# Up-projections and three branches of a gated merge are put into a queue of filling work

## The chip, the cores and the metric

The kernel runs on one NeuronCore of a Trainium2 chip. It has five engines that run side by side and wait for each other through semaphores: TensorE (PE, matrix products), VectorE (DVE), ScalarE (ACT), GpSimd (POOL) and SyncE (SP, which issues most of the transfers). The 16 DMA engines move data between HBM and the on-chip memory. The metric is the device time of one execution in microseconds (us); lower is better.

## The reference, cut to what matters

Two blocks are chained over a sequence of 1024 tokens and a model width of 1024. The first is a hybrid layer: one normalised input h feeds four branches of width 256 (a gated delta rule, "dn"; an attention with low-rank queries and keys, "mla"; a gated linear attention, "gla"; an attention with forget gates, "fox"), and a gated merge adds them up:

```python
cq = rms_norm(mla_cq, mla_q_norm)
b_q = (cq @ mla_w_q_up).reshape(b_sz, s_len, HEADS, MLA_NOPE + MLA_ROPE)
ckv = rms_norm(mla_ckv, mla_kv_norm)
b_kv = (ckv @ mla_w_kv_up).reshape(b_sz, s_len, HEADS, MLA_NOPE + MLA_V)
...
for i in range(N_BRANCHES):
    gate = jax.nn.sigmoid(h @ w_gate[i] + b_gate[i])
    merged = merged + gate * (branches[i] @ w_branch_up[i])
x = x + rms_norm(merged @ w_out, norm_mix_post)
```

An MLP follows. The second block starts from a recurrence over a separate context of 256 tokens (ctx), which needs nothing of the first block:

```python
hk = rms_norm_2(ctx, norm_g[l]) * (1.0 + scale_k) + shift_k
vk = jnp.einsum('btd,de->bte', hk, lp['w_in'][:, :BRANCH_W])
_, state_k = rglru(vk, lp, h0)
```

`rglru` is a short convolution, two gates, a decay and a scan, in two directions. Its end state starts the scan over the 1024 tokens later on.

## The kernel before, in words

Every dense product is made of three matmuls, since each operand is split into a rounded high part and the rest as a low part: hi·hi, hi·lo, lo·hi (`mm3_steps`, lines 411 to 413). A tile is 128 rows by 512 columns of one PSUM buffer; names say which pool it is from: `mm` (two buffers, and a third in turn outside the attentions) and `pp` (five). Weights come as raw tiles `wr` (128x1024, 512 KB), which ScalarE casts to `wh` (line 367) and VectorE subtracts to `wl` (line 368); three of each exist. Tiles of 128x1024 ("S") exist 32 times.

The stages are emitted one after the other: the input norm and `h`, the rows of gates, the projections of mla (`mla_proj`), the queue (`fillers`), the two attentions, the delta rule in two halves (`dn_half`), `gla`, a load ahead of the first merged branch (`prefetch`), the context path (`ctx`), the merge, the product with w_out, the MLP, and the mixers of the second block.

Two things set the order of instructions on each engine. The first is the queue of filling work, `self.fill`: generators of dense products from h that nobody needs yet, in this order: the dn projections (two halves), the gla projections, and `rest`, the products of all four gates (4 branches by 8 blocks by 48 matmuls, whose results go through a tanh to HBM as `gt`). The stages call `W(us)` wherever TensorE would wait; it takes steps off the queue until the credit of so many us is used up (one step of three matmuls of 512 columns counts 0.64), and `need(name)` runs what is left of one entry. The second is a scheduler that reorders instructions by readiness; what it gives is a fixed order on every engine, so that an instruction which waits holds up all that stands behind it on its engine.

In `mla_proj`, `up(i)` makes the 4 blocks of queries by 2 halves (8 pieces of 6 matmuls), then come 4 pieces of keys (3 matmuls) and 8 of values (3 short matmuls of 256 columns). The results are split and stored to HBM by `stage` through tiles `sth`, `stl` and `vst` (a pool of 6). `attention` reads them back.

In the context path `cx` is the loaded context; squares of it are summed over partitions by a matmul with ones (line 463), and it becomes `kh`, `kl`. Then four chunks: a weight tile (`xw`, `xwh`, `xwl`), 24 short matmuls, a copy `cv`, the convolution on VectorE, the split into `xh`, `xl`, 12 short matmuls with `abh`, `abl` (6 for each direction). After the chunks come decays and scans. Between the parts, `W(WC * us)` puts filling work.

`merge` goes over the branches in the order 3, 1, 0, 2. For each of 16 units of a branch it loads the gate `g`, makes 6 matmuls from `br`, multiplies on VectorE (line 1346) and adds into `ma` (line 1348, on VectorE or GpSimd). Branch 2 also splits each sum into `m`.

Of the kernel before, what the change touches and what calls it, by code (L numbers as in the profile page):

```python
# [9 lines left out]
F32R = mybir.dt.float32r  # L10
# [7 lines left out]
P = 128  # L18
# [9 lines left out]
WA, WB, WD, WI, WL, WS, WH, WG, WC = 1.2, 0.7, 10, 18, 0.6, 0.7, 3, 1.2, 2  # L28
# [273 lines left out]
class Build:  # L302
# [517 lines left out]
    def mla_proj(self):  # L820
# [38 lines left out]
        wq = self.load_w(self.A["wq"])  # L859

        def up(i):
            return lambda epi: self.proj(self.cols(wq, 2, 512, i), cq, epi)
# [14 lines left out]
        for hp in range(2):  # L877
            self.mla_k.append(self.stage("mk", lambda epi: self.proj(self.cols(wk, 1, 512, hp), ck, epi)))
        self.mla_v, epi = self.stage_v("mlav")
        for tb in range(8):  # L880
            hf, tl = divmod(tb, 4)
            ts = slice(tl * P, tl * P + P)
            ps = self.mm()
            self.mm3(ps[:, 0:256], [(ck.hi(0, hf)[:, ts], ck.lo(0, hf)[:, ts], wk[0][:, 256:512], wk[1][:, 256:512])])
            epi(ps, tb)

# [270 lines left out]
    def gla(self):  # L1157
        nc = self.nc
        M = nc.tensor.matmul
        self.need("gla")  # L1160
        vn = [self.S("vn") for _ in range(2)]
# [150 lines left out]
    def prefetch(self):  # L1312
        self.brs = [self.branch(b) for b in MERGE[:1]]

    def merge(self):

        nc = self.nc
        acc = Pairs(8)
        self.m = HiLo.__new__(HiLo)
        self.m.t = [None, None]  # L1320

        def finish(n, hf):
            self.hilo(acc.get(n, hf), self.m.hi(n, hf), self.m.lo(n, hf))

        last = None
        brs = self.brs
        for i, b in enumerate(MERGE):
            br = brs.pop(0)
            if i < 3 and not brs:
                brs.append(self.branch(MERGE[i + 1]))  # L1330
            for g in range(2):
                w = self.take("wup", b, g)
                split = i == 3 and g == 1
                for n, hf in sorted(((4 * g + j, hf) for j in range(4) for hf in range(2)),
                                    key=lambda v: v[::-1] if split else v):
                    c = [slice(k * HALF + (n % 4) * P, k * HALF + (n % 4) * P + P) for k in range(2)]
                    if i == 0:
                        acc.alloc(self, hf, "ma")
                    if i == 3 and self.m.t[hf] is None:
                        self.m.t[hf] = [self.S("m", F32R) for _ in range(8)]  # L1340
                    t = self.T2("g")
                    nc.sync.dma_start(t, self.gt[b, n, hf])
                    ps = self.pp() if n % 2 else self.mm()
                    self.mm3(ps, [(w[0][:, c[k]], w[1][:, c[k]], br.hi(k, hf), br.lo(k, hf)) for k in range(2)])
                    a = acc.get(n, hf)
                    nc.vector.scalar_tensor_tensor(t if i else a, t, 1.0, ps, op0=ALU.add, op1=ALU.mult)
                    if i:
                        (nc.vector if i < 3 and (n + hf) % 3 == 0 else nc.gpsimd).tensor_add(a, a, t)
                    if last:
                        finish(*last)  # L1350
                        last = None
                    if i == 3:
                        last = n, hf
        finish(*last)
# [447 lines left out]
    def rg_gates(self, v, N, c):  # L1802
# [7 lines left out]
        for d in range(2):  # L1810
# [13 lines left out]
            yield 3.6 * N / T  # L1824
# [13 lines left out]
    def rg_decay(self, st, N, c):  # L1838

        nc = self.nc  # L1840
        ms = []
        for d in range(2):
            i8 = 4 * d + c
            xc, r, ig, m = st[d]
            m = m if m is not None else self.S("m")
            nc.scalar.activation(m[:, :N], r[:, :N], AF.Tanh, scale=self.SP[:, i8:i8 + 1])
            nc.scalar.activation(r[:, :N], r[:, :N], AF.Exp, scale=self.NSP[:, i8:i8 + 1])
            nc.vector.tensor_mul(ig[:, :N], ig[:, :N], xc[:, :N])
            nc.scalar.activation(xc[:, :N], r[:, :N], AF.Square)
            nc.vector.scalar_tensor_tensor(m[:, :N], xc[:, :N], 1.0, m[:, :N], op0=ALU.add, op1=ALU.mult)  # L1850
            ms.append(m)
            yield 2.3
        return ms

    def rg_scan(self, st, ms, N, init):

        nc = self.nc
        out = []
        for d in range(2):
            xc, a, ig, _ = st[d]  # L1860
            m = ms[d]
            nc.scalar.activation(m[:, :N], m[:, :N], AF.Sqrt)
            nc.vector.tensor_mul(ig[:, :N], ig[:, :N], m[:, :N])
            f = (lambda ap: ap) if d == 0 else (lambda ap: ap[:, ::-1])
            nc.vector.tensor_tensor_scan(f(xc[:, :N]), f(a[:, :N]), f(ig[:, :N]), 0.0 if init is None else init[d],  # L1865
                                         op0=ALU.mult, op1=ALU.add)
            out.append(xc)
            yield 2.4
        return out
# [369 lines left out]
def emit(tc, ctx, A, out, dbg=None, stages=None):  # L2239
# [6 lines left out]
             ("mla", B.mla_proj), ("g0", B.fillers),  # L2246
             ("fox", B.attention), ("dn0", lambda: B.dn_half(0)),
             ("dn1", lambda: B.dn_half(1)), ("gla", B.gla),
             ("merge", B.prefetch),
# [35 lines left out]
```

## Time and profile before

| what | value |
|---|---|
| median of 3 runs | 2550.22 us (2545.32 to 2559.27) |
| profiled execution | 2546.38 us |
| its span | 2544.6 us |
| TensorE busy | 2462.2 us (97%), 12692 matmuls |
| VectorE busy | 1726.1 us (68%) |
| ScalarE busy | 1193.8 us (47%) |
| GpSimd busy | 181.9 us (7%) |
| TensorE's idle time put down to waits | largest: 10.1, 8.8, 6.5, 5.1 us by line |

The span is the part of the execution that the profiler covers; the profiled execution took 1.8 us more than it. TensorE is the bound almost everywhere, so that the time can be read as TensorE's work plus the places where it waits, or runs at a lower clock. PEclk in a window's row is the granted clock as a share of full speed, 2.4 GHz; 0.50 is the lower level, 1.2 GHz.

### The profile page before, as it was taken

What the parts mean: (1) busy time and instruction counts of PE and PEld (TensorE: products, weight loads), DVE (VectorE), ACT (ScalarE), POOL (GpSimd) and SP (SyncE); (2) the same over time, 40 slices, a digit from 0 to 9 for tenths busy, and PEclk for the clock granted to TensorE, in tenths of its full rate; (3) what the DMA queues carried; (4) which work ended last, traced back from release to release, by engine and by line L of the source; (5) the groups of instructions that cost most, each with busy time, mean ns of one, the idle gap of its engine ahead of it and who ended that gap; (6) DMA issues with size and microseconds to landing.
All of it is one profiled execution on the core that took longest, in us unless ns stands there. A gap on an engine that the chain in (4) does not pass through costs nothing. (4 is left out here: it accounts for less than half of the span.)

```text
span 2544.6 us, 33697 instructions
## 1 busy us (share of the span) xinstructions
PE 2462.2 (97%) x12692; PEld 1996.6 (78%) x12692; DVE 1726.1 (68%) x2647; ACT 1193.8 (47%) x1848; POOL 181.9 (7%) x238
## 2 busy tenths in 40 slices
PE   8989999999989999999999999999999999999997
PEld 6878898777777678877788888887888888887786
DVE  7537566574755436758867864468798999996744
ACT  6425554622514358146744543435536355445623
POOL 0000000120211111630000000000000000000000
PEclk9989999999999999999999999999999999999999
DMA  6364453584774567859676565556533333325732
GB/s 223 105 212 138 129 152 114 163 242 118 218 220 145 184 208 235 301 174 281 229 263 223 173 212 169 195 184 229 186 117 113 133 134 98 112 92 195 243 100 100
DMA packets 180084, 449.23 MB, mean 177 GB/s; under 512 B 32144, under 2 KB 42256, under 8 KB 179920
## 3 DMA queue, kind: packets, MB, share of 16 engines
q1 hardware_dynamic: 141504, 342.44, 40.7%
q0 software_dynamic: 18576, 64.63, 9.2%
q10 hardware_dynamic: 19840, 40.00, 4.2%
q8 instruction: 100, 1.64, 0.3%
q14 instruction: 64, 0.52, 0.1%
HBM read 321.55 MB, written 125.44 MB: 176 GB/s over the span
## 5 line engine op out<-in xcount | busy, mean ns | idle before, releaser
L367 ACT CAST wh<-wr 128x1024 fp32r<-128x1024 f32 (+1 forms) x243 | 254.8, 1049 | 481.6 <-PE mm L412 231.1
L368 DVE TENSOR_TENSOR wl<-wr,wh 128x1024 fp32r<-128x1024 f32 (+1 forms) x243 | 298.6, 1229 | 180.9 <-ACT wh L367 172.4
L411 PE MATMUL mm<-h,wh 128*128 128x512 f32 x736 | 301.2, 410 | 7.1 <-ACT h L467 4.3
L412 PE MATMUL mm<-h,wh 128*128 128x512 f32 x736 | 298.0, 405 | 0.0
L413 PE MATMUL mm<-h,wl 128*128 128x512 f32 x736 | 295.9, 402 | 0.3 <-DVE wl L368 0.3
L411 PE MATMUL mm<-kk,wh 128*128 128x512 f32 x704 | 275.2, 391 | 0.0
L412 PE MATMUL mm<-kk,wh 128*128 128x512 f32 x704 | 274.5, 390 | 0.5 <-DVE kk L1784 0.5
L413 PE MATMUL mm<-kk,wl 128*128 128x512 f32 x704 | 274.0, 389 | 0.0
L411 PEld LDWEIGHTS mm<-h,wh 128*128 128x128 f32 x736 | 141.8, 193 | 39.7 <-ACT h L467 5.9
L412 PEld LDWEIGHTS mm<-h,wh 128*128 128x128 f32 x736 | 141.8, 193 | 32.4 <-issue 3.6
L1994 DVE SCALAR_TENSOR_TENSOR pp<-cu,vec,pp 128x512 f32<-128x512 f32 (+9 forms) x240 | 166.7, 749 | 0.1
L413 PEld LDWEIGHTS mm<-h,wl 128*128 128x128 f32 x736 | 141.1, 192 | 32.6 <-issue 1.8
L412 PEld LDWEIGHTS mm<-kk,wh 128*128 128x128 f32 x704 | 132.1, 188 | 29.2 <-issue 1.0
L411 PEld LDWEIGHTS mm<-kk,wh 128*128 128x128 f32 x704 | 132.1, 188 | 28.3 <-issue 0.7
L413 PEld LDWEIGHTS mm<-kk,wl 128*128 128x128 f32 x704 | 132.1, 188 | 27.6 <-issue 0.2
L1512 PE MATMUL pp<-h,wh 128*128 128x512 f32 x320 | 127.1, 400 | 3.0 <-ACT x L1579 2.2
L1513 PE MATMUL pp<-h,wh 128*128 128x512 f32 x320 | 125.0, 391 | 1.4 <-DVE h L468 1.4
L1514 PE MATMUL pp<-h,wl 128*128 128x512 f32 x320 | 123.9, 390 | 0.0
L1721 PE MATMUL pp<-bl,wh 128*128 128x512 f32 x304 | 119.3, 392 | 2.3 <-DVE bl L468 1.6
L1722 PE MATMUL pp<-bh,wl 128*128 128x512 f32 x304 | 118.4, 389 | 0.0
L1720 PE MATMUL pp<-bh,wh 128*128 128x512 f32 x304 | 116.4, 391 | 1.6 <-ACT bh L472 1.6
L411 PE MATMUL mm<-cx,wh 128*128 128x512 f32 x256 | 99.8, 391 | 1.3 <-ACT cx L467 1.3
(559 smaller groups left out, 5453.2 us busy)
## 6 DMA issues: line engine op xcount, KB each, us to landing
wr<-in_wi_dram SPq DMA_DIRECT2D x77, 512.0 KB, 3.7
ws<-in_wm_dram POOLq DMA_DIRECT2D x48, 512.0 KB, 5.9
wr<-in_wo_dram SPq DMA_DIRECT2D x48, 512.0 KB, 3.7
wr<-in_wg_dram SPq DMA_DIRECT2D x32, 512.0 KB, 4.6
gt<-gt POOLq DMA_DIRECT2D x64, 256.0 KB, 3.6
g<-gt SPq DMA_DIRECT2D x64, 256.0 KB, 5.2
wm<-in_wm_dram SPq DMA_DIRECT2D x32, 512.0 KB, 5.0
br<-buB SPq DMA_DIRECT2D x32, 512.0 KB, 4.5
```

The costliest lines, as they stand in the source:

```text
L367: self.nc.scalar.copy(hi, raw)
L368: self.nc.vector.tensor_sub(lo, raw, hi.bitcast(F32))
L411: M(ps, lhsT=ah, rhs=bh, start=start and i == 0, stop=False)
L412: M(ps, lhsT=ah, rhs=bl, start=False, stop=False)
L413: M(ps, lhsT=al, rhs=bh, start=False, stop=stop and i == last)
L1512: M(ps, lhsT=ah, rhs=bh, start=start and i == 0, stop=False, skip_group_check=True)
L1513: M(ps, lhsT=ah, rhs=bl, start=False, stop=False, skip_group_check=True)
L1514: M(ps, lhsT=al, rhs=bh, start=False, stop=i == last, skip_group_check=True)
L1720: M(banks[p], lhsT=wh[:, o], rhs=bh[:, r], start=first, stop=False, skip_group_check=True)
L1721: M(banks[p], lhsT=wh[:, o], rhs=bl[:, r], start=False, stop=False, skip_group_check=True)
L1722: M(banks[p], lhsT=wl[:, o], rhs=bh[:, r], start=False, stop=jj == 7 and e == 1, skip_group_check=True)
L1994: nc.vector.scalar_tensor_tensor(o, u[:, a + s:b + s], w(j), o, op0=ALU.mult, op1=ALU.add)
```

## The change: what it does

There are four edits. The queue is set up inside `mla_proj`, ahead of the up-projections, and each of the 20 pieces is followed by `W(1.4)`; the pieces now use the `pp` buffers. The merge becomes a generator, `merge_steps(i)`, one step for each unit; those of the first three branches are one more entry at the end of the queue, put there at the start of `gla`. The load ahead (`prefetch`) is gone, and the branches are loaded where they start, or by `ahead_of`. The constants of the credits differ: WI (delta rule) 18 to 21, WC (context) 2 to 1.7, and the context's own shares. Two kinds of ScalarE instruction of the context are kept in program order.

```diff
-WA, WB, WD, WI, WL, WS, WH, WG, WC = 1.2, 0.7, 10, 18, 0.6, 0.7, 3, 1.2, 2
+WA, WB, WD, WI, WL, WS, WH, WG, WC, WU = 1.2, 0.7, 10, 21, 0.6, 0.7, 3, 1.2, 1.7, 1.4
...
         wq = self.load_w(self.A["wq"])
+        self.fillers()
+        self.att = True
+
+        def between(w, x, epi):
+
+            for hf in range(2):
+                ps = self.pp()
+                self.mm3(ps, [(w[0][k], w[1][k], x.hi(k, hf), x.lo(k, hf)) for k in range(len(x))])
+                epi(ps, HS[hf], hf)
+                self.W(WU)
 
         def up(i):
-            return lambda epi: self.proj(self.cols(wq, 2, 512, i), cq, epi)
+            return lambda epi: between(self.cols(wq, 2, 512, i), cq, epi)
...
-            ps = self.mm()
+            ps = self.pp()
             self.mm3(ps[:, 0:256], [(ck.hi(0, hf)[:, ts], ck.lo(0, hf)[:, ts], wk[0][:, 256:512], wk[1][:, 256:512])])
             epi(ps, tb)
+            self.W(WU)
...
         self.need("gla")
+        self.fill["merge"] = self.merge_fill()
...
-    def prefetch(self):
-        self.brs = [self.branch(b) for b in MERGE[:1]]
-
-    def merge(self):
+    def merge_steps(self, i):
...
-                    ps = self.pp() if n % 2 else self.mm()
+                ps = self.pp() if n % 2 and i > 1 else self.mm()
...
+                yield 1.3
+        if last:
+            finish(*last)
+
+    def ahead_of(self, i):
+
+        if i not in self.brs:
+            self.brs[i] = self.branch(MERGE[i])
+
+    def merge_fill(self):
+        for i in range(3):
+            yield from self.merge_steps(i)
+
+    def merge(self):
+        self.ahead_of(3)
+        self.need("merge")
+        run(self.merge_steps(3))
...
-            yield 3.6 * N / T
+            yield 3.6 if N == T else 2.4
...
-            yield 2.3
+            yield 2.3 if N == T else 1.2
...
-            yield 2.4
+            yield 2.4 if N == T else 1.2
...
-             ("mla", B.mla_proj), ("g0", B.fillers),
+             ("mla", B.mla_proj),
...
-             ("merge", B.prefetch),
```

The order of instructions shows it at three places. The first is TensorE in the projections of mla, where a row is line, operation, output, stationary and moving operand and shape; `cn` are the normalised low-rank queries and keys, `h` the filling work. Before, the last piece of queries is followed by the first piece of keys:

```order
L411 MATMUL mm_1338<-cn_880,wh_1247 128x512
L412 MATMUL mm_1338<-cn_880,wh_1247 128x512
L413 MATMUL mm_1338<-cn_880,wl_1248 128x512
L411 MATMUL mm_1362<-cn_976,wh_1356 128x512
L412 MATMUL mm_1362<-cn_976,wh_1356 128x512
L413 MATMUL mm_1362<-cn_976,wl_1357 128x512
```

In the changed kernel there is filling work on both sides of a piece:

```order
L412 MATMUL mm_1273<-h_124,wh_1269 128x512
L413 MATMUL mm_1273<-h_124,wl_1270 128x512
L411 MATMUL pp_1283<-cn_879,wh_1247 128x512
L412 MATMUL pp_1283<-cn_879,wh_1247 128x512
L413 MATMUL pp_1283<-cn_879,wl_1248 128x512
L411 MATMUL pp_1283<-cn_880,wh_1247 128x512
L412 MATMUL pp_1283<-cn_880,wh_1247 128x512
L413 MATMUL pp_1283<-cn_880,wl_1248 128x512
L411 MATMUL mm_1273<-h_125,wh_1269 128x512
```

Before, all 84 matmuls with `cn` stand together, and 35 with `h` stand behind the last of them and ahead of the first attention's; now 126 with `h` stand among the 84 and 6 behind the last.

The second place is TensorE at the first chunk of the context path, where `xh`, `xl` are the split result of the convolution and `kh`, `kl` the normalised context. Before, filling work stands between the chunk's projection and its gates:

```order
L412 MATMUL mm_9403<-h_132,wh_9182 128x512
L413 MATMUL mm_9403<-h_132,wl_9183 128x512
L411 MATMUL pp_8959<-xh_8955,abh_8936 128x256
L411 MATMUL pp_8964<-xh_8955,abh_8936 128x256
L411 MATMUL mm_9403<-h_133,wh_9182 128x512
L412 MATMUL mm_9403<-h_133,wh_9182 128x512
L412 MATMUL pp_8959<-xl_8956,abh_8936 128x256
L413 MATMUL pp_8959<-xh_8955,abl_8937 128x256
```

In the changed kernel the projection's last matmul is followed by the gates at once:

```order
L412 MATMUL pp_9154<-kl_9130,xwh_9150 128x256
L413 MATMUL pp_9154<-kh_9129,xwl_9151 128x256
L411 MATMUL pp_9217<-xh_9213,abh_9182 128x256
L411 MATMUL pp_9222<-xh_9213,abh_9182 128x256
L412 MATMUL pp_9217<-xl_9214,abh_9182 128x256
L413 MATMUL pp_9217<-xh_9213,abl_9183 128x256
L412 MATMUL pp_9222<-xl_9214,abh_9182 128x256
L413 MATMUL pp_9222<-xh_9213,abl_9183 128x256
```

In the changed kernel the last matmul of the gates' products (`h`) stands ahead of the first chunk, and none from there to the end of the first 6 of the second chunk's gates: 24 with `kh`, 12 with `xh`, 24 with `kh`, 6 with `xh`. Only then the first matmul of the merge comes (`br`); 114 of its 384 stand among the remaining pieces of the context, 1 to 24 at a place, and 270 behind the last. Behind the last matmul of gla there were 98 with `h`, the two sums of line 463, and 59 more ahead of the first chunk; now there are 66, the sums, and 44.

The third place is the transfers that SyncE issues between gla and the context path (`bo` stores of gla's output, `br` loads of a merged branch, `cx` loads of the context). Before:

```order
L325 DMA bo_8742<-bo_8739 128x1024
L325 DMA br_8749<-bo_2314 128x1024
L325 DMA bo_8747<-bo_8744 128x1024
L325 DMA br_8750<-bo_3117 128x1024
L325 DMA br_8751<-bo_2319 128x1024
L325 DMA br_8752<-bo_3122 128x1024
L1876 DMA cx_8833<-in_ctxT_dram 128x1024
```

In the changed kernel:

```order
L325 DMA bo_8997<-bo_8994 128x1024
L1907 DMA cx_9079<-in_ctxT_dram 128x1024
L1907 DMA cx_9081<-in_ctxT_dram 128x1024
L325 DMA bo_9002<-bo_8999 128x1024
L372 DMA wr_9730<-in_wup_dram 128x1024
L372 DMA wr_9853<-in_wup_dram 128x1024
```

The loads of the context no longer stand behind those of a branch, and the branch's four loads stand further down, behind the loads for the second chunk.

## Rows read from the trace of the kernel before

**Rows 1.** The head of the page.

```profile
span 2544.6 us, 33697 instructions
```

**Rows 2.** Waits of TensorE: line, releaser: us in all, times, longest us.

```profile
PE pp L1020 <- DMA TT<-dT: 10.1, 2, 8.2
PE pp L463 <- DVE acc L462: 8.8, 2, 4.8
...
PE mm L411 <- DVE g L1346: 4.3, 1, 4.3
```

**Rows 3.** Windows: us; PE, PEld, DVE, ACT, POOL busy (x); PEclk, DMA, GB/s.

```profile
143.80:181.60 37.80, 28.44 (x112) 22.54 (x111) 17.47 (x28) 11.64 (x22) 1.08 (x2) 0.82 0.94 296
...
1025.00:1050.00 25.00, 25.00 (x112) 20.71 (x111) 16.72 (x24) 1.06 (x1) 16.11 (x11) 1.00 0.94 341
```

**Rows 4.** TensorE by line, 143.7 to 181.5 us: xcount, busy us, mean ns, idle.

```profile
L411 PE MATMUL mm<-cn,wh 128*128 128x512 f32 x20 | 8.0, 401 | 2.2 <-DVE stl L468 2.2
...
L411 PE MATMUL mm<-h,wh 128*128 128x512 f32 x9 | 4.7, 521 | 2.8 <-DVE vst L468 2.8
...
L411 PE MATMUL mm<-wh,cn 128*128 128x256 f32 x8 | 3.6, 446 | 4.3 <-DVE stl L468 4.3
```

**Rows 5.** Windows where the context path begins, same columns.

```profile
930.00:935.00 5.00, 1.05 (x4) 0.82 (x3) 4.00 (x8) 4.44 (x10) 0.00 (x0) 0.78 1.05 318
935.00:940.00 5.00, 5.00 (x14) 3.86 (x14) 1.95 (x6) 4.05 (x7) 1.08 (x2) 0.54 0.76 225
```

**Rows 6.** Timeline of SyncE there (start us, us, engine, line, op, names).

```profile
916.28 2.87 SPq L325 DMA_DIRECT2D br<-bo  x3
919.55 0.86 SPq L1876 DMA_DIRECT2D cx<-in_ctxT_dram  x2
```

**Rows 7.** Timeline of TensorE there, with its idle time and releaser.

```profile
929.78 0.39 PE L413 MATMUL mm<-h,wl 128*128 128x512 f32 x1
934.12 1.19 PE L463 MATMUL pp<-acc,ones 128*128 128x256 f32 x2 [3.95 <-DVE acc L462]
```

**Rows 8.** Timeline of ScalarE before the first context projection.

```profile
948.09 1.05 ACT L367 CAST wh<-wr 128x1024 fp32r<-128x1024 f32 x1 [1.47 <-PE mm L412]
...
949.62 1.04 ACT L367 CAST xwh<-xw 128x1024 fp32r<-128x1024 f32 x1
```

**Rows 9.** Timeline of VectorE in the same place.

```profile
949.17 1.22 DVE L368 TENSOR_TENSOR wl<-wr,wh 128x1024 fp32r<-128x1024 f32 x1 [2.04 <-ACT wh L367]
950.69 1.23 DVE L368 TENSOR_TENSOR xwl<-xw,xwh 128x1024 fp32r<-128x1024 f32 x1 [0.30 <-ACT xwh L367]
...
959.02 0.76 DVE L468 TENSOR_TENSOR xl<-rg,xh 128x256 fp32r<-128x256 f32 x2
```

**Rows 10.** Timeline of TensorE and ScalarE at the first context chunk.

```profile
954.59 0.28 PE L412 MATMUL pp<-kl,xwh 128*128 128x256 f32 x1
...
954.71 0.28 PE L413 MATMUL pp<-kh,xwl 128*128 128x256 f32 x1
...
958.19 0.41 ACT L467 CAST xh<-rg 128x256 fp32r<-128x256 f32 x1
```

**Rows 11.** VectorE by line from 1013 to 1095 us, the merge.

```profile
L1346 DVE SCALAR_TENSOR_TENSOR g<-g,mm 128x512 f32<-128x512 f32 x22 | 14.7, 679 | 6.2 <-DMA g<-gt 6.2
...
L468 DVE TENSOR_TENSOR m<-ma,m 128x512 fp32r<-128x512 f32 x10 | 9.6, 959 | 4.9 <-ACT m L467 4.9
L1348 DVE TENSOR_TENSOR ma<-ma,g 128x512 f32<-128x512 f32 x10 | 8.9, 894 | 0.3
```

**Rows 12.** Windows of the context path and of the merge's start.

```profile
950.00:975.00 25.00, 25.00 (x141) 21.40 (x140) 15.37 (x30) 19.84 (x36) 3.62 (x6) 1.00 0.71 232
975.00:1000.00 25.00, 25.00 (x149) 22.29 (x148) 13.28 (x31) 24.74 (x45) 4.14 (x7) 1.00 0.69 204
1000.00:1025.00 25.00, 23.58 (x103) 18.84 (x102) 22.47 (x43) 13.34 (x23) 0.89 (x1) 1.00 0.95 315
```

**Rows 13.** Table loads of ScalarE at one line, whole span.

```profile
L1833 ACT ACT_TABLE_LOAD x9 | 11.5, 1283 | 0.2
```

More of the change, by code (lines that the diff above doesn't have):

```diff
@@ L877, in mla_proj @@
         for hp in range(2):
-            self.mla_k.append(self.stage("mk", lambda epi: self.proj(self.cols(wk, 1, 512, hp), ck, epi)))
+            self.mla_k.append(self.stage("mk", lambda epi: between(self.cols(wk, 1, 512, hp), ck, epi)))
         self.mla_v, epi = self.stage_v("mlav")
@@ L1310, in branch @@
         return br
-    def prefetch(self):
-        self.brs = [self.branch(b) for b in MERGE[:1]]
-    def merge(self):
+    def merge_steps(self, i):
         nc = self.nc
-        acc = Pairs(8)
-        self.m = HiLo.__new__(HiLo)
-        self.m.t = [None, None]
+        b = MERGE[i]
+        if i == 0:
+            self.macc, self.brs = Pairs(8), {}
+        if i == 3:
+            self.m = HiLo.__new__(HiLo)
+            self.m.t = [None, None]
+        acc = self.macc
+        self.ahead_of(i)
+        br = self.brs.pop(i)
         def finish(n, hf):
@@ L1325, in merge @@
         last = None
[L1326 to L1342, printed above, removed]
-                    ps = self.pp() if n % 2 else self.mm()
[L1344 to L1353, printed above, removed]
@@ L1354, in merge @@
-        finish(*last)
+        for g in range(2):
+            w = self.take("wup", b, g)
+            split = i == 3 and g == 1
+            for n, hf in sorted(((4 * g + j, hf) for j in range(4) for hf in range(2)),
+                                key=lambda v: v[::-1] if split else v):
+                c = [slice(k * HALF + (n % 4) * P, k * HALF + (n % 4) * P + P) for k in range(2)]
+                if i == 0:
+                    acc.alloc(self, hf, "ma")
+                if i == 3 and self.m.t[hf] is None:
+                    self.m.t[hf] = [self.S("m", F32R) for _ in range(8)]
+                t = self.T2("g")
+                nc.sync.dma_start(t, self.gt[b, n, hf])
+                ps = self.pp() if n % 2 and i > 1 else self.mm()
+                self.mm3(ps, [(w[0][:, c[k]], w[1][:, c[k]], br.hi(k, hf), br.lo(k, hf)) for k in range(2)])
+                a = acc.get(n, hf)
+                nc.vector.scalar_tensor_tensor(t if i else a, t, 1.0, ps, op0=ALU.add, op1=ALU.mult)
+                if i:
+                    (nc.vector if i < 3 and (n + hf) % 3 == 0 else nc.gpsimd).tensor_add(a, a, t)
+                if last:
+                    finish(*last)
+                    last = None
+                if i == 3:
+                    last = n, hf
+                yield 1.3
@@ L1356, in add_sq @@
+        if last:
+            finish(*last)
+    def ahead_of(self, i):
[8 more added lines that the diff above has]
+        run(self.merge_steps(3))
     def add_sq(self, acc, x, first):
@@ L1845, in rg_decay @@
             m = m if m is not None else self.S("m")
-            nc.scalar.activation(m[:, :N], r[:, :N], AF.Tanh, scale=self.SP[:, i8:i8 + 1])
+            i = nc.scalar.activation(m[:, :N], r[:, :N], AF.Tanh, scale=self.SP[:, i8:i8 + 1])
+            if N < T:
+                self.tc.keep_in_program_order(i)
             nc.scalar.activation(r[:, :N], r[:, :N], AF.Exp, scale=self.NSP[:, i8:i8 + 1])
@@ L1861, in rg_scan @@
             m = ms[d]
-            nc.scalar.activation(m[:, :N], m[:, :N], AF.Sqrt)
+            i = nc.scalar.activation(m[:, :N], m[:, :N], AF.Sqrt)
+            if N < T:
+                self.tc.keep_in_program_order(i)
             nc.vector.tensor_mul(ig[:, :N], ig[:, :N], m[:, :N])
```

## The prediction

> **What bounds the kernel now.** I read the windows first, then TensorE's waits, then the timelines where a wait is long. In a dense stretch TensorE starts 112 matmuls of 512 columns in 25 us [rows 3], so one costs 25/112 = 0.223 us; one of 256 columns follows the last by 0.12 us [rows 10]. TensorE is busy nearly throughout, so the reader should look for places where a window has fewer starts than that, or a clock under 1.00, and not for the busiest engine.
>
> Three such places bear on the change. The first is the stage of the mla projections: 37.8 us at a clock of 0.82, with the DMA engines busy 0.94 of the time at 296 GB/s [rows 3]. It holds 60 + 26 matmuls of 512 columns and 24 of 256 [rows 4] (of each three kinds the rows show one; the others have 20, 20; 9, 8; 8, 8), that is 86 x 0.223 + 24 x 0.12 = 22.1 us of work. So 15.7 us are lost: 2.2 + 2.8 + 4.3 = 9.3 us in waits for the split tiles `stl` and `vst`, whose stores are late, and 6.4 us in matmuls that run at the lower clock (means 521 and 446 ns against 401 [rows 4]).
>
> The second is the start of the context path: TensorE waits 3.95 us for the sum of squares [rows 7], since the context's load was issued at 919.55, right behind three loads of a branch [rows 6]. The 5 us after that wait have 14 starts at a clock of 0.54 [rows 5], where a dense stretch has 22.4: another 8.4 x 0.223 = 1.9 us, and some 0.4 us before that.
>
> The third is the merge: a wait of 4.3 us for VectorE [rows 2] with about 1.9 us of lower clock after it (priced by rows 5), and 103 starts instead of 112 in the window from 1000 us, 2.0 us, where VectorE is busy 22.47 of 25 us [rows 12]. That is 8.2 us in all.
>
> **The change, part by part.**
>
> Filling between the up-projections. Nothing is added: the 132 matmuls stood later in the queue. A piece is now followed by 6 to 7 of them, so that a piece of queries (two stores of 256 KB) comes each 2.8 us instead of back to back. Stores and loads of the stage are 296 GB/s x 37.8 us = 11.2 MB; the extra weights make it at most 12.2 MB. The stage's work is now 22.1 + (132 - 26) x 0.223 = 45.7 us, and at the rate that the rows show at full DMA use, 296/0.94 = 315 GB/s, 12.2 MB take 38.7 us. So stores keep up, with 7 us to spare, and most of the 15.7 us goes. I take off 12: what is late next is the weight tile of the keys, which needs the buffer of the last query weight. Ends: -15.7, all of it, and -3, if bursts still fill the six store tiles.
>
> The context's load. It no longer stands behind a branch, and goes out about when the second last output of gla is stored, some 13 us earlier in this order; 66 matmuls (14.7 us) stand in front of its sum. The wait of 3.95 us and the slow clock behind it, 2.3 us, go: -6.3 us. Ends: -6.3 and 0.
>
> The first two context chunks. Here the order takes the cover away: the filling work that stood there now runs earlier, in the mla stage and in the delta rule, and the queue is dry when the first chunk starts. Three waits appear that the trace of before shows only as distances between instructions:
> (1) The projection of chunk 0 needs `xwh` and `xwl`. On ScalarE their cast stands behind the cast of another weight that needs a buffer held by the last `h` matmul. The same sequence is in the trace: that cast starts at 948.09 when TensorE lets go of the buffer, `xwh` ends at 949.62 + 1.04 = 950.66 [rows 8], `xwl` at 950.69 + 1.23 = 951.92 [rows 9]. The third matmul of the projection needs `xwl`, so TensorE stands still for 951.92 - 948.09 = 3.8 us. Before, 59 matmuls with `h` ran there.
> (2) The gates of chunk 0 need `xh`: the projection's last matmul starts at 954.71 and takes 0.28 us, the cast of the first `xh` ends at 958.19 + 0.41 = 958.60 [rows 10], and its `xl` at about 959.4, half way through the pair that starts at 959.02 [rows 9]. That is 3.6 us before the two matmuls that need `xh` alone and some 0.6 us behind them: 4.2.
> (3) Chunk 1 repeats it: 4.2.
> Together 12.2 us. Each wait is as long as the one at 930 us, behind which the clock fell, so each costs 2.1 us more: 6.3. I take +18.5. The order of TensorE is fixed, and behind the waiting instruction stand the second chunk and the whole merge. Ends: +6, if two of the three waits are covered after all, and +24, with one as long as the longest that rows show, 8.2 us, the other two at 4.8 [rows 2], and the clock's 6.3.
>
> The merge among the context's pieces. From the first `br` matmul to the last, TensorE has 384 x 0.223 + 78 x 0.12 = 95 us. VectorE has 64 products at 0.68 = 43.5, 10 sums at 0.89 = 8.9 and 16 splits at 0.96 = 15.4 [rows 11], 7 weight splits at 1.23 [rows 9] = 8.6, and the rest of the context. That is about two chunks, decays and scans: 15.37 less two weight splits, and 13.28 less one [rows 12], together 25. The sum is 101 us. So VectorE has more to do than TensorE, in a stretch where branches 3 and 1 have three PSUM buffers instead of eight: TensorE can be three units of 1.34 us ahead, no more. The loss of 8.2 us becomes 101 - 95 = 6 plus the same end of branch 2, about 5: I take +3. Ends: -4 (the early 2.0 and some of the clock go) and +12 (below).
>
> The delta rule. WI puts 176 matmuls in front of the first half's wait for `TT` (175 before) and 179 in the second's (172): 7 x 0.223 = 1.6 us off the longest wait of 8.2 us [rows 2]; the filling ahead of the second half's first `th` falls from 104 to 95, 2.0 us more there. I take 0, ends -3 and +2.
>
> ScalarE's table loads: nine fewer in the order, at 1283 ns each [rows 13], 11.5 us of ScalarE. In the window from 975 us ScalarE is busy 24.74 of 25 us and TensorE 25.00 [rows 12], so they end nothing there; 0. The Trainium skill (ScalarE: Activation LUTs, What ACT_TABLE_LOAD costs) adds a drain of about 1.38 us to each switch, 2.66 us in all; by that, nine fewer would be worth 24 us of ScalarE, and if ScalarE set the pace of the decays, up to that much of the time. No row here shows such a drain, and TensorE has no gap there.
>
> Sum: -12 - 6.3 + 18.5 + 3 + 0 = +3.2 on the profiled execution's 2546.4 (span 2544.6 [rows 1] and 1.8 around it) = 2549.6. The median of the runs shown is 3.8 us above that execution; the sum's own error is larger, and I forecast 2550.
>
> **Rivals.**
>
> Faster: the waits at the context's start are mostly covered. For it: the context's load and with it `kh` come earlier, and the DMA engines are no longer at 1.05 there [rows 5]. Against it: the order has no filling work at all between the chunks, and the three waits are chains of ScalarE and VectorE work on TensorE's own result. Price: +6 instead of +18.5, the merge at 0: 2546.4 - 12 - 6.3 + 6 = 2534, and 2527 with both savings at their ends.
>
> Slower: VectorE sets the pace of the merge. In its first 25 us it was busy 22.47, 0.90 [rows 12]; at that share 101 us of work take 112, 17 more than TensorE's 95, and with the end of branch 2 about 20 where 8.2 were lost: +12. With the waits at their upper end: 2546.4 - 12 - 6.3 + 24 + 12 = 2564. It decides from the point where the merge's waits for `g` pass some 10 us. For it: three PSUM buffers, and the context's decays stand in the same queue of VectorE as the products that free them. Against it: GpSimd takes most sums, and TensorE's own waits give VectorE time.
>
> No gain in the mla stage: the DMA engines stay at 0.9 and more, and the stores still hold TensorE up. Price: -3 instead of -12, 2559. For it: 12.2 MB in 45.7 us is 85% of the rate seen. Against it: the waits are for single tiles, and the pieces now come evenly.
>
> **How the numbers follow.** No change can be told within 0.5%, that is 2537.5 to 2563 about the median. The forecast has 0.40 (own range 2541 to 2560), the faster rival 0.30, the slower one 0.20, the mla rival 0.10. Faster by over 0.5%: most of 0.30 and a tail of the forecast, 0.31. Slower: 0.15 from the slower rival, which lies about the bound, and 0.08 from the tails of the forecast and the mla rival: 0.23. Same: 0.46. The range takes in both outer rivals but for their tails: 2526 to 2568.
>
> **What would show it.** In the new profile: the waits for `stl` and `vst` gone and the clock at 1.00 in the mla stage (first step); no wait of line 463 at the sum of squares there (second); three idle times of 3 to 5 us ahead of the first `kh`, `xh` and second `xh` matmuls, with windows of clock near 0.5 between (third); VectorE over 0.9 busy from the first `br` on, and waits for `g` of line 1357 (fourth). The forecast is wrong by a whole sign if the third is absent, or if the fourth is over 10 us.

## The result, and the profile after

The changed kernel takes 2570.3 us (median of 7 runs, 2565.2 to 2575.7); the kernel before, run beside it, 2550.1 (7 runs, 2542.4 to 2560.9). The ratio is 1.0078, 95% interval 1.0060 to 1.0097: slower by 0.8%. That is beyond the 0.5% that can be told from no change, and 2 us above the predicted range. The profiled execution took 2573.8 us.

To see where, I split both profiles at the same pieces of work. The table gives what each stage lost or won: its length, less 0.227 us (the distance of two matmuls in a dense stretch) for each matmul of 512 columns in it that the order can move, against the same of the kernel before. So a stage that merely received filling work shows 0.

| stage of TensorE (us, + is lost) | predicted | after | after, second profile | before, second profile |
|---|---|---|---|---|
| up to the first score of attention (mla stage) | -12 | -17.0 | -15.2 | -0.9 |
| attention and delta rule | 0 | -5.7 | -4.3 | +0.3 |
| gla | – | +11.1 | +17.2 | +3.0 |
| last of gla to the context's first `kh` matmul | -6.3 and +3.8 | -4.3 | -4.3 | +0.1 |
| context path, first `kh` to last `xh` | +14.7 | +29.6 | +27.2 | 0.0 |
| rest of the merge, to the first matmul with `m` | +3 | +1.8 | +2.9 | -2.7 |
| first to last matmul with `m` (out_proj) | – | +10.9 | +11.3 | +1.2 |
| rest | 0 | +1.1 | +2.1 | -0.3 |
| sum | +3.2 | +27.4 | +36.9 | +0.9 |

(Of the predicted +18.5 at the context's start, 3.8 us were the first wait, which lies ahead of the first `kh`.) The second profiles, of 2583.3 and 2547.7 us, repeat every stage within 3 us, except the changed kernel's gla. So a difference of a few us in one stage of one profile is not yet an effect.

TensorE's waits in the changed kernel, whole span (line, releaser: us in all, times, longest us):

```profile
PE pp L411 <- ACT xh L467: 13.2, 4, 3.7
PE pp L1013 <- ACT th L1010: 7.8, 4, 2.5
PE mm L411 <- DVE g L1357: 6.5, 5, 3.2
PE mm L411 <- ACT h L467: 4.3, 1, 4.3
PE pp L463 <- DVE acc L462: 4.2, 1, 4.2
PE mm L413 <- DVE wl L368: 4.2, 1, 4.2
PE pp L1031 <- DMA TT<-dT: 3.4, 1, 3.4
...
PE pp L411 <- ACT xwh L367: 2.4, 1, 2.4
PE pp L1031 <- DMA T<-dT: 2.4, 1, 2.4
```

Against [rows 2], the two waits for `TT` (10.1 us) have become one of 3.4 and one of 2.4 for `T`, the context's wait for the sum of squares is gone (the one of line 463 that is left lies elsewhere), and four waits for `xh` stand at the top.

Windows of the changed kernel (columns as in [rows 3]): the mla stage, the end of gla, the context path, the middle of the merge, and its end.

```profile
141.90:188.60 46.70, 46.70 (x219) 39.01 (x219) 19.76 (x30) 15.31 (x28) 1.08 (x2) 1.00 0.76 249
...
960.00:1040.00 80.00, 61.32 (x278) 50.80 (x278) 44.17 (x82) 35.77 (x69) 3.70 (x5) 0.83 0.60 197
1040.00:1090.00 50.00, 45.77 (x193) 36.64 (x192) 48.97 (x72) 14.46 (x25) 30.43 (x21) 0.97 0.78 259
1090.00:1110.00 20.00, 17.68 (x76) 13.64 (x75) 15.14 (x18) 7.29 (x11) 13.72 (x10) 1.00 0.70 228
1110.00:1130.00 20.00, 13.37 (x42) 9.08 (x41) 14.45 (x17) 7.10 (x11) 12.07 (x9) 0.74 0.25 89
881.00:936.00 55.00, 55.00 (x290) 38.28 (x290) 11.30 (x17) 22.53 (x31) 3.35 (x6) 0.81 0.15 50
```

The mla stage is dense: TensorE busy for all 46.7 us at a clock of 1.00, the DMA engines at 0.76 where they were at 0.94 [rows 3]. The context path is the opposite: in 80 us TensorE is busy 61.3, and the clock is 0.83. From 1040 us VectorE is busy 48.97 of 50 us and TensorE 45.77.

The context path on TensorE's timeline (start us, us, line, names, idle before and releaser), only the longer waits:

```profile
964.92 0.58 PE L411 MATMUL pp<-kh,xwh 128*128 128x256 f32 x1 [2.43 <-ACT xwh L367]
...
966.18 0.58 PE L413 MATMUL pp<-kh,xwl 128*128 128x256 f32 x1 [0.46 <-DVE xwl L368]
...
974.95 0.80 PE L411 MATMUL pp<-xh,abh 128*128 128x256 f32 x2 [3.71 <-ACT xh L467]
...
984.78 0.56 PE L411 MATMUL pp<-xh,abh 128*128 128x256 f32 x2 [3.59 <-ACT xh L467]
...
985.62 0.58 PE L412 MATMUL pp<-xl,abh 128*128 128x256 f32 x1 [0.28 <-DVE xl L468]
...
1003.67 0.50 PE L411 MATMUL pp<-xh,abh 128*128 128x256 f32 x2 [2.81 <-ACT xh L467]
...
1024.42 0.50 PE L411 MATMUL pp<-xh,abh 128*128 128x256 f32 x2 [3.04 <-ACT xh L467]
...
1030.32 0.77 PE L411 MATMUL mm<-br,wh 128*128 128x512 f32 x1 [2.02 <-DMA br<-bo]
```

The first three are those that the prediction worked out. Those at 1003 and 1024 us, of the third and fourth chunk, it did not have. Behind each wait matmuls run at the lower clock level in this profile: the same matmul with `kh` and `xwh` takes 0.41 us at 969 us and 0.28 at 979:

```profile
968.91 0.41 PE L413 MATMUL pp<-kh,xwl 128*128 128x256 f32 x1
969.12 0.41 PE L411 MATMUL pp<-kh,xwh 128*128 128x256 f32 x1
...
979.23 0.28 PE L411 MATMUL pp<-kh,xwh 128*128 128x256 f32 x1
979.35 0.28 PE L412 MATMUL pp<-kl,xwh 128*128 128x256 f32 x1
```

The end of the merge, VectorE first, then TensorE:

```profile
1120.65 1.09 DVE L468 TENSOR_TENSOR m<-ma,m 128x512 fp32r<-128x512 f32 x1 [1.21 <-ACT m L467]
1121.67 0.68 DVE L1357 SCALAR_TENSOR_TENSOR g<-g,pp 128x512 f32<-128x512 f32 x1
1122.27 1.21 DVE L368 TENSOR_TENSOR wl<-wr,wh 128x1024 fp32r<-128x1024 f32 x1
1123.40 2.58 DVE L468 TENSOR_TENSOR m<-ma,m 128x512 fp32r<-128x512 f32 x2
```

```profile
1123.54 0.79 PE L413 MATMUL mm<-m,wl 128*128 128x512 f32 x1 [4.16 <-DVE wl L368]
1124.13 0.63 PE L411 MATMUL mm<-m,wh 128*128 128x512 f32 x1
1124.56 0.63 PE L412 MATMUL mm<-m,wh 128*128 128x512 f32 x1
```

VectorE is still multiplying gates (`g`) and splitting `m` when out_proj already wants the split weight `wl`, which stands behind them in its queue. The cast that `wl` needs comes late as well: on ScalarE it starts at 1120.53, behind casts of `m` that wait up to 2.3 us each for GpSimd's sums. TensorE waits 4.16 us and then starts a matmul each 0.43 us, at the lower level.

### The profile page after: what moved, and what is told of

Same layout as the page of the kernel before. It is cut to its first block, busy times and chain, and to the rows that moved or that the text cites. A ratio compares the mean times of both kernels' runs of the same rounds, so it can differ in the third digit from the quotient of the medians.

```text
span 2571.9 us, 33682 instructions
## 1 busy us (share of the span) xinstructions
PE 2480.8 (96%) x12692; PEld 2004.3 (78%) x12692; DVE 1734.4 (67%) x2647; ACT 1183.2 (46%) x1839; POOL 181.2 (7%) x238
## 5 line engine op out<-in xcount | busy, mean ns | idle before, releaser
L367 ACT CAST wh<-wr 128x1024 fp32r<-128x1024 f32 x243 | 255.0, 1049 | 490.2 <-PE mm L412 260.0
L368 DVE TENSOR_TENSOR wl<-wr,wh 128x1024 fp32r<-128x1024 f32 x243 | 298.9, 1231 | 211.3 <-ACT wh L367 202.2
```

The costliest lines, as they stand in the source:

```text
L367: self.nc.scalar.copy(hi, raw)
L368: self.nc.vector.tensor_sub(lo, raw, hi.bitcast(F32))
```

## The experiments

Two theories were set against each other. **C (cover)**: the loss is at the context's start, because the filling between the up-projections took what covered it; the merge in the queue costs little. **D (merge)**: the loss is the merge as filling work, since VectorE and three PSUM buffers pace it. Each experiment names its edit against the kernel before or the changed one; all were timed beside the kernel before (median 2548.9 to 2550.5).

**The filling between the up-projections alone** (the kernel before, with `WU` = 1.4):

```diff
+                self.W(WU)
...
-            return lambda epi: self.proj(self.cols(wq, 2, 512, i), cq, epi)
+            return lambda epi: between(self.cols(wq, 2, 512, i), cq, epi)
...
-              ("mla", B.mla_proj), ("g0", B.fillers),
+              ("mla", B.mla_proj),
```

> The kernel before with the filling work between the up-projections alone; queue, merge and constants otherwise as before. Theory C (the slowdown is lost cover: the filling work spent early is missing at the context's chunks): 15 us gained in the mla stage, and the gates of the second, third and fourth chunk stand bare in the order, three waits of 3 to 4 us with 1.5 to 2 us of slow clock each, so about 2551 us (2546 to 2556), no change against before. Theory D (the slowdown is VectorE and three PSUM buffers in the merge that runs inside the context): the merge is the old one, so the 15 us stay, 2535 to 2540 us.

Measured: 2569.0 us (6 runs, 2555.9 to 2572.3), ratio 1.0072 (1.0048 to 1.0095). Both missed: this half of the change alone is as slow as the whole. By stage: mla -16.8, gla +14.5, context +25.0, rest of the merge -5.1, out_proj +1.2. Its three waits for `xh`, at the second to fourth chunk, are longer than the changed kernel's (timeline of TensorE):

```profile
991.82 1.36 PE L411 MATMUL pp<-xh,abh 128*128 128x256 f32 x3 [4.31 <-ACT xh L467]
...
1005.64 1.36 PE L411 MATMUL pp<-xh,abh 128*128 128x256 f32 x3 [5.76 <-ACT xh L467]
...
1018.44 0.80 PE L411 MATMUL pp<-xh,abh 128*128 128x256 f32 x2 [4.82 <-ACT xh L467]
```

So C is right that the context loses its cover, and too low on the price: +25.0 there is more than the mla stage's gain of 16.8. But the context does not make this kernel slow by itself. The other large loss, gla's +14.5, is in neither theory; the clock over that stage is 0.74 (855.9 to 932.2 us), where the kernel before has 0.95.

**The merge in the queue alone** (the changed kernel without the filling between the up-projections):

```diff
-        def between(w, x, epi):
...
-            self.W(WU)
...
+              ("mla", B.mla_proj), ("g0", B.fillers),
```

> The changed kernel with the up-projections as before (no filling between them): merge in the queue, new constants, context loaded ahead of the branch. Theory C: the order has filling work in every gap of the context, so no wait there, the early wait of 4 us for the sum of squares gone: 2545 us (2540 to 2552). Theory D: branches 3 and 1 still have three buffers and VectorE the context's scans between: 2556 to 2562 us.

Measured: 2578.8 us (2571.0 to 2586.2), ratio 1.0118 (1.0097 to 1.0140). Both missed again. By stage: attention and delta rule +9.8, gla +21.3, context +6.8, out_proj +0.4. The context, with its cover left, loses a quarter of what the changed kernel loses there: that part of C holds. But with this half the merge's end costs nothing either, so the +10.9 of the changed kernel comes from neither edit alone. And gla, which this edit touches only by which filling work is left for it, is the worst of all. It starts with a wait of 3.81 us for `kt`, and from there the clock is at the lower level for 44 us:

```profile
862.00:902.00 40.00, 39.17 (x228) 24.59 (x229) 10.49 (x24) 3.29 (x5) 2.17 (x4) 0.50 0.31 93
```

TensorE is busy 39.17 of 40 us at a granted clock of 0.50; 29 of its 228 matmuls there have 512 columns, the others 64 or 128. The parts do not add: 20 and 30 us alone, 20 together.

**Eight PSUM buffers for all merged branches**:

```diff
-                ps = self.pp() if n % 2 and i > 1 else self.mm()
+                ps = self.pp() if n % 2 else self.mm()
```

> The changed kernel, where every second unit of all merged branches takes one of the five other PSUM buffers, as before the change. Theory C: the first two chunks stay bare, only the waits of the third and fourth chunk (6 us) and for g (6.5 us) can shrink: 2564 us (2560 to 2569). Theory D: the merge keeps ahead of VectorE and the end of the merge loses nothing: 2550 to 2558 us.

Measured: 2563.2 us (2556.8 to 2567.1), ratio 1.0053 (1.0033 to 1.0074), as C had it. The merge's waits for `g` stay (7.1 us, where the changed kernel has 6.5), so it is not more buffers that they lack; out_proj falls to +7.5, but the rest of the merge rises to +6.4, so that the two lose 13.9 where the changed kernel lost 12.7. The context falls from +29.6 to +25.5: the order now puts 7 and 5 matmuls with `br` between the `kh` and `xh` of the third and fourth chunk, where the changed kernel has 1 and 0. So three buffers do take cover from the context. That this is what makes the kernel 7 us faster is not shown: the changed kernel's second profile has +27.2 there, and gla (+6.6) and the delta rule (-9.3 with attention) are lower in this profile too.

**The context's norm ahead of gla's last output**, so that `kh` is ready earlier (the function is split, and `ctx_norm` called in gla):

```diff
+        self.ctx_norm()
...
-    def ctx_path(self):
+    def ctx_norm(self):
+        run(self.modg)
...
+        self.kx = hh, hl
```

> The changed kernel, where the context's load, sum of squares and normalisation are emitted inside gla, ahead of its outputs, so that the filling work that is left stands between the parts of chunks 0 and 1. Theory C: the waits before the first projection (3.4 us) and the first two gates (7.8 us) go with their slow clock: 2554 us (2549 to 2560). Theory D: only the merge's end counts, and VectorE has the same work there: 2567 to 2571 us.

Measured: 2563.8 us (2558.0 to 2564.7), ratio 1.0053 (1.0034 to 1.0073), between the two. The context falls from +29.6 to +18.4: the order has 25 and 18 matmuls with `h` between the `kh` and `xh` of the first two chunks, where the changed kernel has none, and two of the four waits for `xh` are gone (6.1 us left). This fall of 11 us is well beyond what the second profile differs by. out_proj keeps +11.3.

**Both together** (early norm and eight buffers):

> The changed kernel with both: the context's normalisation inside gla and eight PSUM buffers for all merged branches. If the two costs are separate their gains add: 2570 - 6.5 - 7 = 2556 us (2552 to 2560). If both only move the same wait along: 2562 to 2565 us, as each alone.

Measured: 2553.6 us (12 runs, 2542.0 to 2563.0), ratio 1.0005 (0.9987 to 1.0023): level with before. Context +13.8, the end of the merge +6.5 and +5.8. Between the changed kernel and this one the median falls by 16.7 us, where the two edits alone took 7.1 and 6.5 off: the gains add up, and a little more.

**The kernel before and the changed kernel once more**, one run each, to see which stages repeat (the table above):

> The kernel before, once more. Theory E (gla is a bistable place: its many short matmuls leave the clock where it is on entry, and the change makes it enter at the low level more often): its own gla stage also varies from run to run, some 43 us beside the filling work when it stays warm, as in the first profile, and up to 60 us when not; total 2542 to 2560 us as its runs so far. Rival (the order alone fixes it): gla as in the first profile within 2 us.

> The changed kernel once more, for its gla stage. Theory E: gla's net time varies between the two profiles by several us, and the waits of the context and of the merge's end do not: 30 and 12 us above the kernel before, within 3 us. Rival: the stages are as fixed as the order, gla too, within 2 us of the first profile.

Measured: 2547.7 and 2583.3 us. gla moves by 3.0 and 6.1 us, more than the 2 us of the rival, while the context and the end of the merge stay within 3 us: that part of theory E holds. That the clock stays in gla as it is on entry does not: in the changed kernel's first profile it is at 0.50 five times between 855 and 934 us, and at 1.00 in between.

**Filling between the quarters of gla's output**, against the lower clock in gla:

```diff
+                    if i < 3:
+                        self.W(0.7)
-                self.head_norm_gate(po, self.vec("gla_norm"), zs[hp], outs[hp], sl)
+                self.head_norm_gate(po, self.vec("gla_norm"), zs[hp], outs[hp], sl, 0.9)
```

> The changed kernel, where gla's filling work is spread between its short matmuls (three of 512 columns behind each quarter of an output) instead of standing in blocks of 12 to 16 behind them; the same amount. Theory E (stretches of 8 us of short matmuls drop the clock): gla at a clock near 1.00, 8 to 11 us less, 2560 us (2556 to 2564). Rival (the clock of gla is set elsewhere): 2567 to 2573 us.

Measured: 2569.5 us (9 runs, 2559.9 to 2581.2), ratio 1.0070 (1.0047 to 1.0092): no gain over the changed kernel. In its profiled run gla, from 844.6 to 921.2 us, stood at 1.00 from 860 on (from 845 to 855 at the lower level):

```profile
860.00:935.00 75.00, 75.00 (x436) 51.56 (x436) 23.25 (x40) 36.41 (x54) 7.24 (x12) 1.00 0.41 126
```

But that run is the fastest of the nine, and the median did not move. Inconclusive: the clock in gla differs from run to run of one kernel, and there is no profile of a middling run. That stretches of short matmuls by themselves bring the clock down is not shown either.

**Early norm with the old merge** (the first experiment and `ctx_norm` in gla):

> The kernel before with the filling work between the up-projections and the context's normalisation inside gla; the merge stands behind the context as before, and is not in the queue. Theory C: the filling work left covers chunks 0 to 2, so the context loses 8 to 12 us instead of 25 and the merge nothing: 2569 - 15 = 2554 us (2547 to 2559). Rival (the uncovered chunk only moves to a later one): 2564 to 2570 us.

Measured: 2553.8 us (12 runs, 2549.3 to 2570.0), ratio 1.0012 (0.9994 to 1.0030), in C's range, but not for C's reason. The context, which was to lose 8 to 12 us, loses 21.6, hardly less than in the first experiment (25.0). What fell most in the profiles is gla, from +14.5 to -2.7, with a clock of 0.97 over the stage where the first experiment had 0.74. So that the total came out as C had it is luck. The rest of the merge has -1.5, out_proj +0.1. Against it, the same stretch of the merge with early norm and eight buffers; first the old merge, then the merge as filling work:

```profile
1030.00:1090.00 60.00, 60.00 (x266) 49.56 (x265) 44.88 (x61) 8.89 (x11) 39.40 (x29) 1.00 0.84 279
```

```profile
1035.00:1095.00 60.00, 49.73 (x209) 38.97 (x208) 54.33 (x77) 11.92 (x22) 37.35 (x26) 0.98 0.71 241
```

With the old merge VectorE is busy 44.9 of 60 us and TensorE all of it; with the merge in the queue VectorE 54.3 and TensorE 49.7.

Three attempts on that part, all on top of early norm and eight buffers: the split of `m` two units behind its product; only the first merged branch in the queue; all sums on GpSimd.

```diff
-                if last:
-                    finish(*last)
...
+                if len(last) > 2:
+                    finish(*last.pop(0))
```

> The kernel with early normalisation and eight buffers (2553.6 us), where the last branch splits each sum two units behind its product instead of one. If the merge's end is paced by the chain product, sum on GpSimd, cast, split, with VectorE waiting in it: 6 to 8 us less there, 2547 us (2542 to 2551). If VectorE's amount of work paces it: no change, 2552 to 2556 us.

```diff
-        for i in range(3):
-            yield from self.merge_steps(i)
+        yield from self.merge_steps(0)
...
```

> The kernel with early normalisation and eight buffers, where only the first merged branch is in the queue and the other two come behind the context. If the merge's end loses 12 us because merge products queue on VectorE behind the context's decays and scans: most of it goes, 2543 us (2539 to 2549). If it is the sum of VectorE's work: 2552 to 2556 us.

```diff
-                    (nc.vector if i < 3 and (n + hf) % 3 == 0 else nc.gpsimd).tensor_add(a, a, t)
+                    nc.gpsimd.tensor_add(a, a, t)
```

> The kernel with early normalisation and eight buffers, where all sums of the merge run on GpSimd: 9 us of work less on VectorE. If VectorE's amount of work paces the merge: 2545 us (2541 to 2550). If not, or if GpSimd becomes the bound: 2552 to 2560 us.

Measured: 2558.9 us (2542.3 to 2564.4), ratio 1.0014 (0.9997 to 1.0032); 2552.7 (2546.0 to 2559.7), 1.0004 (0.9992 to 1.0016); 2557.3 (2549.7 to 2562.7), 1.0026 (1.0012 to 1.0039). None beats the kernel that it started from (2553.6); the first lies above both of its expectations, the other two where "no gain" had them. With the split two units later VectorE's waits for the cast of `m` at the end of the merge fall from 4.3 to 1.2 us, and out_proj loses 8.9 all the same. With one branch in the queue out_proj loses nothing more (0.0 for +5.8), but the rest of the merge loses 10.2 for 6.5, 7.8 us of it in one wait that ends at `H`, VectorE's copy of the end state of a scan of the context:

```profile
PE mm L411 <- DVE H L1948: 7.8, 1, 7.8
```

With all sums on GpSimd the waits for `g` halve (4.0 us for 8.9) and others grow (4.8 us for 1.1 at `H`, 4.6 for 3.6 at `wl`). So less work on VectorE did not help here; that the order of what stands in its queue (scans, splits of weights, products) decides is likely, but GpSimd's longer chain of sums (busy 47.93 of 60 us for 37.35) is a rival that stays. No version ran clearly faster than the kernel before.

## Why the prediction was wrong, point by point

**The mla stage: right, at its upper end.** Predicted -12 with an end of -15.7; measured -17.0, of which -1.7 lie ahead of the stage. The waits for `stl` and `vst` are gone and the clock is 1.00, as foreseen; the late weight tile of the keys for which I held back 3.7 us shows no wait. The third rival (no gain here) is refuted, and by the first experiment with the same -16.8. (One reading of mine was loose: the mean of 446 ns is of matmuls of 256 columns, 0.28 us each in a dense stretch [rows 10], and not to be set against the 401 of 512 columns. The 6.4 us do not hang on it. And the faster rival's 2527 does not follow from its terms: 2546.4 - 15.7 - 6.3 + 6 is 2530.)

**The context's load: right.** No wait at its sum of squares; SyncE issues it behind a store of gla (timeline of SyncE):

```profile
935.78 0.92 SPq L325 DMA_DIRECT2D bo<-bo  x2
936.76 2.81 SPq L1907 DMA_DIRECT2D cx<-in_ctxT_dram  x2
```

The stage's -4.3 holds the new wait of 2.43 us; without it it is -6.7, for -6.3 predicted.

**The context chunks: the step that failed, and the largest error of what the sum held.** Predicted +18.5, measured 2.4 + 29.6 = +32.0, above its upper end of 24. The mechanism was right: ScalarE's timeline has the sequence of [rows 8] again, to 0.02 us in the two casts:

```profile
962.30 1.04 ACT L367 CAST wh<-wr 128x1024 fp32r<-128x1024 f32 x1 [1.15 <-PE mm L412]
...
963.83 1.03 ACT L367 CAST xwh<-xw 128x1024 fp32r<-128x1024 f32 x1
```

And the three waits that I priced at 12.2 us measured 2.43 + 0.46, 3.71 and 3.59 + 0.28 = 10.5. What I got wrong is where they stop. The prediction named "the first two context chunks", since the first `br` matmul comes behind them, and took the rest as covered. The order says how many stand between the `kh` and the `xh` of a chunk, and for the third and fourth that is 1 and 0. So these wait too, 2.81 + 0.15 + 3.04 = 6.0 us, and 2.0 more go to the load of `br`. The other 13.5 us (32.0 - 10.5 - 8.0) are lower clock, where I had 6.3 for three waits (the clock is 0.82 over the 73 us of the stage, which is 13 us lost): with one wait each 10 to 20 us the clock is 0.73, 0.76, 0.83 in three successive windows of 10 us from 960 on. This size does not repeat: in the second profile the stage and its first wait lose 29.6, the waits are 20.3 of that, and 9.3 are left; behind the first wait of 2.43 us its matmuls run at full speed. The experiments show the cause of the stage's loss: with the filling left in place it is 6.8, with the filling moved and the old merge 25.0, and cover brought back by the early norm takes 11 us off.

**The merge: +3 predicted, +12.7 measured** (1.8 + 10.9), just past its upper bound of +12. It is in part the slower rival's mechanism, VectorE at 0.98 busy from 1040 to 1090 us (not from the first `br` on, as I had it: from 960 to 1040 it is 44.17 of 80), with less than its price in waits for `g` (6.5 us, where I had set 10 as the point from which it decides) and the rest at a place that I did not look at: out_proj, with 6.6 us of waits for `wl` and `m`, and the lower level from 1118 to 1128 us. From the first matmul with `m` to the last split of `m` it took 13.3 us before and 16.8 after. I had worked out VectorE's 101 us against TensorE's 95, and let the difference end with the merge.

The 101 us were also too low. The context's decays and scans, which I priced from the kernel before, took VectorE longer in the changed kernel (VectorE by line, 960 to 1095 us, one of four kinds of instruction, before and after):

```profile
L1863 DVE TENSOR_TENSOR rg<-rg 128x256 f32<-128x256 f32 x8 | 3.3, 421 | 1.6 <-ACT rg L1862 1.3
```

```profile
L1894 DVE TENSOR_TENSOR rg<-rg 128x256 f32<-128x256 f32 x8 | 7.9, 990 | 0.0
```

The four kinds together, 32 instructions, took 15.3 us before and 23.4 after. Before, no sum of GpSimd ran beside any of them. In the changed kernel the merge's sums do, and each instruction that takes longer than before has one beside it (timeline of VectorE and GpSimd):

```profile
1055.55 0.41 DVE L1894 TENSOR_TENSOR rg<-rg 128x256 f32<-128x256 f32 x1
...
1057.24 2.93 POOL L1359 TENSOR_TENSOR ma<-ma,g 128x512 f32<-128x512 f32 x2 [3.10 <-DVE g L1357]
...
1059.01 1.44 DVE L1894 TENSOR_TENSOR rg<-rg 128x256 f32<-128x256 f32 x1
```

How much of the stage's loss this is was not tried. Nor is it shown that a backlog on VectorE makes the loss in out_proj: when the last matmul with `br` ends, 6 products are left to VectorE, in the kernel before 4, but in its second profile 6 too, with +1.2 there. That the sum of work on VectorE is the whole cause is made unlikely by the kernel with all sums on GpSimd; what of the order in the queues costs most stays open.

**The delta rule: 0 predicted, -5.7 measured.** The longest wait for `TT` fell from 8.2 to 3.4 us. The order gave 1.6 us more cover there and I took that as all; the waits shrank by more. The credit (WI) is not what does it: with the filling between the up-projections alone, and the old credit, the waits for these transfers are 1.9 us in all; with the merge alone, and the new credit, 12.9. Why they differ so much stays open.

**Gla: not in the sum, +11.1.** I had put it at nothing without a reason. Its only wait, 2.6 us for `kt` at the start, is as long as before (2.5); what differs is the clock. The whole stage in the kernel before, in the changed kernel and in its second profile (windows, columns as in [rows 3]):

```profile
845.20:907.30 62.10, 62.07 (x467) 42.56 (x468) 23.81 (x44) 25.60 (x34) 5.13 (x9) 0.95 0.37 122
```

```profile
854.40:936.50 82.10, 82.10 (x508) 56.21 (x508) 21.03 (x38) 26.61 (x37) 8.13 (x13) 0.83 0.30 84
```

```profile
857.70:945.90 88.20, 88.19 (x507) 60.64 (x508) 21.04 (x38) 26.59 (x37) 8.13 (x13) 0.77 0.27 78
```

A clock of 0.95 over 62.1 us is 3 us lost, 0.83 over 82.1 is 14, and 0.77 over 88.2 is 20: 11 and 17 us more than before, which are the +11.1 and the +17.2. So the clock is the whole of gla's loss. The second profile of the kernel before has +3.0, so most of it goes with the change, but by how much differs from run to run. What brings it on stays open. Each of gla's four outputs is a stretch of 5 to 10 us of matmuls of 64 and 128 columns; the clock was at the lower level in part of one of the four in the first profile of the kernel before, of two in its second, of all four in both of the changed kernel, though TensorE waits in none. The attempt to prevent it did not move the median.

**Table loads: 0, not contradicted.** No wait for a load shows in the merge or the context.

In sum: mla -5.0 against the forecast, delta rule -5.7, context +13.1 with the load, merge +9.7, gla +11.1, the rest +1.1: 24.3 of the 24.2 us between +3.2 and +27.4. The medians are 20 us apart, since the profiled run of the changed kernel is 3.5 us above its median and that of before 3.7 below its own.

## What to carry to other kernels

Filling work that is moved to one gap is taken from another. Before a gain is booked, count in the order how much filling is left between each producer and its consumer, chunk by chunk and to the last, since the matmuls behind a wait can run at the lower clock level, which here cost 13.5 us beside 18.5 us of waits in one profile and 9.3 beside 20.3 in another. Work that itself needs the engine that is busy in a gap (here VectorE's products, scans and splits) is poor filling for it: with it in the gap VectorE was busy 54.3 of 60 us and TensorE 49.7, without it 44.9 and 60. And before a kernel is called slow for one stage's loss, the other stages' share is to be read too: with the merge alone in the queue gla lost 21.3 us, and the context, which the theories were about, 6.8.

## What was not expected of the hardware

TensorE was busy 39.17 of 40 us at a granted clock of 0.50, in gla of the kernel with the merge alone, while the kernel with filling between the quarters stood at 1.00 from 860 us to the end of the same stage. The two stretches do not hold the same work: 29 matmuls of 512 columns in the 40 us there, 67 in the first 40 here, and the first began behind a wait of 3.81 us. So TensorE's busy share does not tell its clock, and the stage differed by 16 us (+21.3 against +5.2). The profiles of one kernel differ by 6 us there (+11.1 and +17.2). The other surprise is VectorE's: the same instruction on 128x256 takes 0.41 us alone and up to 1.44 us beside a sum of GpSimd.
